# Keys' low parts on both halves of the partitions: attention products over full rows in a hybrid three-branch block

## The chip, the cores and the metric

The kernel runs on one core of a Trainium2 chip. The metric is the device time of one execution in microseconds (us), the median of several runs. The core's engines are named as in the profile: PE (TensorE, matrix products; PEld its weight loads), DVE (VectorE), ACT (ScalarE), POOL (GpSimd) and SP (SyncE, which here only issues DMAs).

## The reference

512 tokens behind 16 meta tokens, 1024 features, one layer, float32. Three attention branches read one projection of the normed input; their outputs are gated, projected and summed, and a convolutional gated feed-forward follows.

```python
def _stick_breaking(q, k, v):            # sb: 4 heads of 64
    z = einsum('bqhd,bkhd->bhqk', q, k) * scale
    log_1m_beta = where(key < query, log_sigmoid(-z), 0.0)
    between = cumsum(log_1m_beta, reverse) - log_1m_beta
    w = where(key < query, exp(log_sigmoid(z) + between), 0.0)
def _indexed_sparse_attention(...):      # sp: 4 heads; 132 keys per query, by an index score
    score = einsum('bqj,bqjk->bqk', w_ix, relu(einsum('bqjd,bkd->bqjk', q_ix, k_ix)))
    _, sel = top_k(score, top_k)         # then softmax(q k * scale + bias) over sel, times v
def _differential_attention(...):        # df: 4 heads, two maps each
    p = softmax(q1 k1 * scale + bias) - lam * softmax(q2 k2 * scale + bias)   # times v
merged = sum(sigmoid(g + b) * (y @ w_br)) over the three;  h = h + merged @ w_out
h = h + (silu(conv(u @ w_gate)) * (u @ w_val)) @ w_down
```

## The kernel before

Features lie on partitions, tokens on columns. For float32 accuracy every operand is split in a high part (rounded to the fast type `F32R`) and a low part, and a dense product is three passes: high times high, weights' high times low, weights' low times high (`mm3`). A dense tile is 8 k-tiles in 3 passes for each half of the tokens, with a new 128 x 128 weight tile loaded for every product of 256 to 264 columns.

TensorE runs in the order in which the code emits. `PLAN` gives the order of the dense tiles: projections of the units sb0, sb1 (two stick-breaking heads each), df0 to df3 (one differential head, two maps), sp0, sp1 (two sparse heads), gates, and branch outputs. Between a dense tile's products, generators ("streams") emit the attention's work, when a rough clock kept at emission says that their operands will be there (a margin `SLACK` of 1800 ns). The top-k of the sparse branch (`topk_stream`) runs on DVE beside the sb units. Weights come in chunks of 128 x 1024 on SP's queue (`wr<-wpk`), three buffers deep; ACT makes the high part (`wh`), POOL or DVE the low part (`wl`), which frees the buffer for a later load.

The attention of a unit goes like this. `q_stream` and `k_stream` (lines 635 to 666) split the projected queries and keys and move halves of 64 partitions by DMA on SP's queue (`move`, line 629): each head's queries become high and low parts above each other, (h, l) on 128 partitions; keys become (h0, h0), (h1, h1) and one tile (l0, l1), in `qk` tiles. `scores` (line 728) then makes two products per piece of a query block:

```python
mm(out, q[:, c0:c0 + m], (k0, k1)[e][:, o:o + n], start=True, stop=False)   # 128 rows: (h+l) of q, h of k
mm(out, q[rr, c0:c0 + m], kl[rr, o:o + n], start=False, stop=True)          # 64 rows: h of q, l of k
```

Each of the 16 score heads (2 for each unit; of a df unit the two maps) has pieces of 16 columns (the two meta queries), 144, 272, 400 and twice 264 (the blocks of 128 queries against the keys so far). DVE reads the scores, adding a mask (`smask`, for sb) or the bias (`W`). `value_stream` (line 855) transposes the weights on PE, the meta queries' 2 x 16 (`ws[i]`, tile `pm`) among them, and multiplies them with the values; the first of these products is over the meta keys (`pm,vm`): 64 rows for the paired heads of sb and sp, 96 rows for df.

Of the kernel before, what the change touches and what calls it, by code (L numbers as in the profile page):

```python
# [15 lines left out]
P = 128  # L16
D = 1024
T = 528            # meta tokens and real tokens
NM = 16
Q0 = 14            # first token whose mixer output is needed (the convolution reaches back two)  # L20
TQ = T - Q0        # 514 queries
HQ = TQ - 256      # 258: two meta queries and query blocks 0 and 1
# [11 lines left out]
# columns of the packed small parameters  # L34
# [4 lines left out]
# chunks of [128, 1024] in the packed weights  # L39
# [4 lines left out]
# the mixer's dense products in order: the projections of two heads' worth of a branch, four tiles  # L44
# of gates, half the columns of a branch's output
# [10 lines left out]
def tile_kernel(ctx: ExitStack, tc, hT, wpk, par, bias, yT):  # L56
# [3 lines left out]
    # ------------------------------------------------------------- order of emission  # L60
    # TensorE runs in the order in which its instructions are emitted here: dense products, with
    # the matmuls of other streams of work between them. A rough clock of the engines tells when a
    # stream's operands will be there, so that its matmuls come no earlier.
# [4 lines left out]
    SLACK = 1800    # from an operand's making by the clock to its matmul  # L68
    BSL = 500       # from a bank's last reading by the clock to its next use
    PACE = 12000    # for a round of the top-k  # L70
    TKS = 10000     # from the index part's making to its first product
    PRI = 100       # by how many instructions an evacuation goes ahead
    SET = 2200      # by how much earlier than SLACK the other engines' dependent steps come
    HVW = 1000      # VectorE's handicap against GpSimd for the weights' low parts
    HV = 500        # and for other differences
# [28 lines left out]

    def sub(out, a, b, hv=HV):
        """a - b in SBUF on VectorE, or on GpSimd where that is free sooner"""
        t = clock["P"]
        tv = max(clock["V"], t) + V.cost(out) + hv
        e = G if max(clock["G"], t) + G.cost(out) < tv else V
        e.tensor_tensor(out, a, b, OP.subtract)  # L110
# [16 lines left out]
    # ------------------------------------------------------------------ pools  # L127
# [13 lines left out]
    def bank(tag):  # L141
        """a PSUM bank, when one is free by the clock"""
        while sum(h["t"] + BSL > clock["P"] for h in held[tag]) >= banks[tag]:
            yield
        h = {"t": math.inf}
        held[tag].append(h)
        return ps.tile([P, 512], F32, tag=tag, bufs=banks[tag], name="ps" + tag), h
# [4 lines left out]
    # Slots that several streams of work share. A slot is taken here before the instructions  # L152
    # that fill it are emitted and given back after the last that reads it is, so an engine that
    # runs in the order of emission can't wait for one that is given back later.
    caps = {"tmp": 13, "qk": 10, "v": 2, "y": 8, "W": 3, "pt": 6, "ptm": 2}
# [29 lines left out]
    # ------------------------------- streams, which run between a dense product's matmuls  # L185
# [14 lines left out]
    def side_by_side(gens):  # L200
        """several streams in one; what each returns"""
# [16 lines left out]
    def settle(more=0):  # L218
        """until what the stream has emitted is done"""
        c = cur[0]  # L220
        while clock["P"] < c["t"] + more + SLACK:
            yield

    def ease(most=3000):
        """while VectorE is far behind"""
# [13 lines left out]
    # -------------------------------------------------------------- constants  # L239
    prm = const.tile([P, NPAR], F32, name="prm")  # L240

    def pc(c):
# [16 lines left out]
    # causal mask of a query block of 128 against columns c, the key at c standing at c - 400  # L259
    # from the block's first query  # L260
    cmask = const.tile([P, T], F32, name="cmask")
    G.memset(cmask, 0.0)
    G.affine_select(cmask, cmask, pattern=[[-1, T]], compare_op=OP.is_ge, fill=NEG, base=400,
                    channel_multiplier=1)
    smask = const.tile([P, T], F32, name="smask")
    G.memset(smask, 0.0)
    G.affine_select(smask, smask, pattern=[[-1, T]], compare_op=OP.is_gt, fill=NEG, base=400,
                    channel_multiplier=1)
    # the two meta queries (14 and 15) against the meta keys
# [4 lines left out]
    # ------------------------------------------------------- weights, streamed  # L274
# [34 lines left out]
    def mm3(out, prs, xh, xl, start=True, stop=True):  # L309
        """out += w^T x for the tiles j of chunk k and k-tiles kt of x, in three exact passes"""  # L310
# [13 lines left out]
    HALF = ((0, TH), (TH, TH))           # all tokens  # L324
    HALQ = ((0, HQ), (HQ, 256))          # queries, counted from token Q0

    # ------------------------------------------------ the input, and its norm's factors
# [16 lines left out]
    # the order that gives TensorE work from the first tile of the input on  # L344
# [21 lines left out]
    def step(k, ds, halves, q0, kt):  # L366
        """one k-tile of a tile of all its columns"""
# [12 lines left out]
    # the first two tiles go along with the input's arrival  # L380
# [17 lines left out]
    def rstd(dst, st, y0, a, now=True):  # L398
        """dst = (v + eps)^-0.5 from st = -v/2 in PSUM: Exp and Ln, then a Newton step"""
# [15 lines left out]
    # ------------------------------------------------ factors from the small parameters  # L415
# [6 lines left out]
    # -lambda of the differential attention on every partition  # L422
# [10 lines left out]
    # ------------------------------------- relative bias, by how far a key lies from the query  # L433
    tab = dram.tile([8, NREL], F32, name="tab")
    gd = [dram.tile([P, NREL], F32, name=f"gd{h}") for h in range(8)]
    braw = const.tile([97, 8 + NREL], F32, name="braw")
    nc.gpsimd.dma_start(braw, bias)

    def bias_stream():
# [3 lines left out]
        for e, r in enumerate(brd):  # L443
            # the table's high and low parts above each other, and the buckets of half the distances
# [14 lines left out]
        # a copy for each query, for the steps along which bias_tile reads  # L459
# [5 lines left out]
    def bias_tile(h):  # L465
        """[p, c]: the bias of query p against the key at column c (that is key c - 400 from the
        block's first query), or -1e30 where the key lies ahead"""
# [5 lines left out]
    # ----------------------------------------------------- dense tile of tokens  # L473
# [14 lines left out]
    # ---------------------------------------------------------------- index part  # L488
# [34 lines left out]
    for g in range(2):  # L523
# [15 lines left out]
        # the high, low and again the high parts of each head above each other, by way of DRAM  # L539
# [7 lines left out]
    # Each query's TOPK keys of the best score. Of the first block's 144 keys, the 144 - TOPK of the  # L547
    # least score are found instead: its scores are kept negated, and from the last key to the
    # first, since of equal scores the later key's counts as the lower.
# [10 lines left out]
    def topk_stream():  # L560
# [40 lines left out]
        # 0 where a key was taken, -1e30 elsewhere  # L601
# [5 lines left out]
    # ----------------------------------- after the projections of a unit of attention  # L607
    def headnorm(raw, n, gain, mat):
        """times gain over the root mean square of the rows that mat groups"""
# [622 lines left out]
```

## Time and profile before

| what | before |
|---|---|
| median of 3 runs | 931.87 us (929.49 to 934.09) |
| span of the profiled execution, first to last instruction | 928.0 us |
| busy in the span | PE 901.2 us (97%), DVE 559.4 (60%), ACT 456.7 (49%), POOL 314.5 (34%) |
| mean granted TensorE clock | 0.996 of full speed |
| weight chunks on SP's queue | 131 of 512 KB, 3.5 us from issue to landing |
| moves of key halves, `qk<-qk` of 132 KB | 24, 3.0 us from issue to landing |

The span is 3.9 us under the median; the two differ by what lies around the first and the last instruction and by the spread of the runs. Ends of products on PE are modelled in the profile, so the cost of a product is read from the starts: from its own to that of the next.

### The profile page before, as it was taken

Reading aid. Unit: us, or ns where it says so; the run is one execution under the profiler, and the core shown is the slowest. Engines: PE = TensorE matmul, PEld = TensorE weight load, DVE = VectorE, ACT = ScalarE, POOL = GpSimd, SP = SyncE. Lnnn points to the kernel's source line nnn. Section 1 sums busy time; section 2 is a strip of 40 time slices with the busy share of each in tenths; the row PEclk is TensorE's granted clock in tenths of the full one; section 3 lists DMA queues with packets and bytes.
Section 4 is the critical chain, followed back from the end, with each engine's and each line's share of the span. In section 5 each row is a group of like instructions: output and inputs, shape, how many; then the busy total and the mean of one; then the engine's idle time right before and its main releaser. Section 6 shows DMA issues by size and latency. Waiting matters only on the chain.

```text
span 928.0 us, 15349 instructions
## 1 busy us (share of the span) xinstructions
PE 901.2 (97%) x6054; PEld 814.3 (88%) x6054; DVE 559.4 (60%) x1129; ACT 456.7 (49%) x848; POOL 314.5 (34%) x185
## 2 busy tenths in 40 slices
PE   7989989899999999999998999999999999999998
PEld 6987988799998889988998999999999999888886
DVE  6599999985578655797437445555555555422221
ACT  7476686668377787644545444333333333311110
POOL 2433232343433424666235323344444333200100
PEclk9999999999999999999999999999999999999999
DMA  6584112142333212331222532223223233333330
GB/s 227 149 237 156 47 69 69 48 125 66 101 104 92 82 63 80 99 97 48 68 78 87 178 91 91 92 91 91 91 91 91 92 96 95 106 113 102 114 102 23
DMA packets 30439, 91.44 MB, mean 99 GB/s; under 512 B 3929, under 2 KB 4073, under 8 KB 30368
## 3 DMA queue, kind: packets, MB, share of 16 engines
q1 hardware_dynamic: 29648, 88.05, 31.0%
q0 software_dynamic: 720, 2.42, 0.9%
q8 instruction: 47, 0.77, 0.3%
q14 instruction: 24, 0.20, 0.1%
HBM read 80.88 MB, written 5.86 MB: 93 GB/s over the span
## 4 chain that ended last, share of the span: by engine, by line
PE 77%; DVE 14%; DMA 4%; ACT 2%; issue 1%; SPq 1%; POOL 0%; DVEq 0%; POOLq 0%; ACTq 0%
PE psd L179 52%; PE psw L179 23%; DVE tmp L97 7%; DVE work L97 2%; DVE m L97 2%; PE psw L183 2%; ACT tmp L97 1%; DMA qd<-tmp 1%; DVE G L97 1%; DMA qk<-qk 1%; DVE pm L97 1%; DMA wr<-wpk 1%; DVE pt L97 1%; DMA qst<-qd 1%; DMA gd<-tab 1%
## 5 line engine op out<-in xcount | busy, mean ns | idle before, releaser
L97 POOL TENSOR_TENSOR wl<-wr,wh 128x1024 fp32r<-128x1024 f32 x75 | 181.3, 2418 | 347.7 <-ACT wh L97 226.7
L97 ACT CAST wh<-wr 128x1024 fp32r<-128x1024 f32 (+2 forms) x137 | 139.2, 1018 | 178.4 <-PE psd L179 123.6
L179 PE MATMUL psd<-xh,wh 128*128 128x258 f32 (+2 forms) x792 | 119.5, 291 | 3.7 <-DVE tmp L97 2.5
L179 PE MATMUL psd<-xh,wl 128*128 128x258 f32 (+2 forms) x792 | 118.6, 290 | 0.0
L179 PE MATMUL psd<-xl,wh 128*128 128x258 f32 (+2 forms) x792 | 118.5, 290 | 0.0
L97 DVE TENSOR_TENSOR wl<-wr,wh 128x1024 fp32r<-128x1024 f32 (+3 forms) x62 | 72.3, 1168 | 69.4 <-PE psd L179 60.2
L179 PEld LDWEIGHTS psd<-xh,wh 128*128 128x128 f32 x792 | 103.8, 189 | 7.5 <-DVE tmp L97 1.8
L179 PEld LDWEIGHTS psd<-xh,wl 128*128 128x128 f32 x792 | 103.1, 189 | 3.3
L179 PEld LDWEIGHTS psd<-xl,wh 128*128 128x128 f32 x792 | 103.5, 190 | 2.9 <-issue 0.2
L97 ACT ACTIVATE tmp<-tmp 128x528 f32<-128x528 f32 (+7 forms) x154 | 69.7, 475 | 23.1 <-DVE tmp L97 20.5
L97 POOL TENSOR_TENSOR ft<-ft 128x512 f32<-128x512 f32 x22 | 46.5, 2115 | 82.5 <-DVE ft L97 79.1
L97 DVE SCALAR_TENSOR_TENSOR ft<-ft,prm 128x512 f32<-128x512 f32 x44 | 58.2, 1324 | 20.3 <-ACT ft L97 19.6
L179 PE MATMUL psw<-qk 128*128 128x400 f32 (+4 forms) x192 | 55.8, 339 | 2.3 <-DVE tmp L97 1.6
L179 PEld LDWEIGHTS psw<-qk 128*128 128x128 f32 (+1 forms) x192 | 32.2, 168 | 19.9 <-issue 6.2
L179 PE MATMUL psw<-uh,wh 128*128 128x256 f32 (+2 forms) x264 | 47.0, 320 | 0.0
L179 PE MATMUL psd<-ul,wh 128*128 128x258 f32 (+2 forms) x264 | 46.9, 319 | 0.0
L179 PE MATMUL psw<-ul,wh 128*128 128x256 f32 (+2 forms) x264 | 46.9, 319 | 0.0
L179 PE MATMUL psd<-uh,wl 128*128 128x258 f32 (+2 forms) x264 | 46.9, 319 | 0.0
L179 PE MATMUL psw<-uh,wl 128*128 128x256 f32 (+2 forms) x264 | 46.8, 319 | 0.0
L179 PE MATMUL psd<-uh,wh 128*128 128x258 f32 (+2 forms) x264 | 46.8, 319 | 0.0
L179 PE MATMUL psd<-ah,wl 128*128 128x512 f32 x176 | 45.6, 395 | 0.0
L179 PE MATMUL psd<-ah,wh 128*128 128x512 f32 x176 | 45.6, 395 | 0.0
(195 smaller groups left out, 1645.8 us busy)
## 6 DMA issues: line engine op xcount, KB each, us to landing
wr<-wpk SPq DMA_DIRECT2D x131, 512.0 KB, 3.5
qk<-qk SPq DMA_DIRECT2D x24, 132.0 KB, 3.0
gd<-tab SPq DMA_DIRECT2D x8, 328.0 KB, 5.2
tmp<-hT SPq DMA_DIRECT2D x8, 264.0 KB, 6.8
W<-gd POOLq DMA_DIRECT2D x8, 264.0 KB, 4.2
qk<-tmp SPq DMA_DIRECT2D x16, 128.5 KB, 2.6
hm<-hT SPq DMA_DIRECT2D x8, 257.0 KB, 3.8
yT<-ft SPq DMA_DIRECT2D x8, 256.0 KB, 2.1
```

The costliest lines, as they stand in the source:

```text
L97: return f(out, *a, **k)
L179: PE.matmul(out, lhsT, rhs, **k)
L183: PE.transpose(out, x, ident[:x.shape[0], :x.shape[0]])
```

## The change

The keys' low parts get the same treatment as the high ones: two tiles, (l0, l0) and (l1, l1), made by three more moves for each unit, and the second product of `scores` runs over all 128 rows (the queries' low part now also meets the keys' low part). A unit holds six `qk` tiles instead of five, and the pool two more. The meta keys' product takes all 96 rows of its tiles, whose other rows are zero. The meta queries' weights live in eight fixed tiles of 128 rows (`pmw`, zero below the second row), and a product with two columns of the identity takes the place of their transpose. One causal mask, a column wider, serves both branches: `smask` is `cmask` read one column on. The raw bias table moves to a slot of the gates' tiles.

```diff
-    caps = {"tmp": 13, "qk": 10, ...}
+    caps = {"tmp": 13, "qk": 12, ...}
-    cmask = const.tile([P, T], F32, name="cmask")
+    cmask = const.tile([P, T + 1], F32, name="cmask")
...
-    smask = const.tile([P, T], F32, name="smask")
-    G.memset(smask, 0.0)
-    G.affine_select(smask, smask, pattern=[[-1, T]], compare_op=OP.is_gt, fill=NEG, base=400, channel_multiplier=1)
+    smask = cmask[:, 1:]
...
-    braw = const.tile([97, 8 + NREL], F32, name="braw")
+    braw = ap_.tile([97, 4, TQ], F32, tag="G", bufs=4, name="braw").rearrange("p a b -> p (a b)")[:, :8 + NREL]
...  k_stream
-        yield from wait("qk", 3)
-        a, b, l = qtile(), qtile(), qtile()
+        yield from wait("qk", 4)
+        a, b, l, m = qtile(), qtile(), qtile(), qtile()
         S.copy(a, raw)
         sub(l, raw, a)
-        move(b[64:128], a[64:128])
-        move(b[0:64], a[64:128])
-        move(a[64:128], a[0:64])
+        for x, y in ((a, b), (l, m)):
+            move(y[64:128], x[64:128])
+            move(y[0:64], x[64:128])
+            move(x[64:128], x[0:64])
...  scores
-        q, (k0, k1, kl) = unit["q"][e], unit["k"]
-        rr = slice(64 * e, 64 * e + 64)
-        mm(out, q[:, c0:c0 + m], (k0, k1)[e][:, o:o + n], start=True, stop=False)
-        mm(out, q[rr, c0:c0 + m], kl[rr, o:o + n], start=False, stop=True)
+        q, kh, kl = unit["q"][e], unit["k"][e], unit["k"][2 + e]
+        mm(out, q[:, c0:c0 + m], kh[:, o:o + n], start=True, stop=False)
+        mm(out, q[:, c0:c0 + m], kl[:, o:o + n], start=False, stop=True)
...  weights of the meta queries
+    pmw = [ap_.tile([P, NM], F32, tag=f"pmw{j}", bufs=1, name=f"pmw{j}") for j in range(8)]
+    for t in pmw:
+        G.memset(t, 0.0)
-            return ap_.tile([2, NM], F32, tag="pm", bufs=8, name="pm")
+            pmw.append(pmw.pop(0))
+            return pmw[-1]
...  value_stream
-                transpose(t[:NM, o:o + m], ws[i][:m, :NM])
+                if i < 0:
+                    mm(t[:NM, o:o + 2], ws[i], ident[:, 0:2], start=True, stop=True)
+                else:
+                    transpose(t[:NM, o:o + P], ws[i][:, :NM])
...
-                mm(y[:, :W], vm[:64, e], pm[:64, :W], start=True, stop=False)
+                mm(y[:, :W], vm[:, e], pm[:, :W], start=True, stop=False)
```

On PE, ACT and DVE the order of the instructions stays what it was, but for four index-score products that come three dense products later, and one weight split that goes from POOL to DVE, both before the first unit's scores; on POOL two loads of bias tiles come a little later among the weight splits. What moves is SP's queue. In it, the moves of df0's keys (`qk` tiles to `qk` tiles of 64 x 528) with the weight loads around them (`wr`) read so before; the words in brackets are what an issue waits for, earlier DMAs (`DMAHW`), PE, ACT or POOL:

```order
L294 DMA wr19_2559<-wpk 128x1024 [waits DMAHW2_49,Pool_49]
L629 DMA qk_2506<-qk_2505 64x528 [waits PE_49,Activation_49]
L629 DMA qk_2506<-qk_2505 64x528
L629 DMA qk_2505<-qk_2505 64x528 [waits DMAHW2_49,DMAHW3_49,DMAHW1_49,Pool_49]
L294 DMA wr20_2621<-wpk 128x1024 [waits DMAHW4_49,Pool_49]
L294 DMA wr51_2740<-wpk 128x1024 [waits Pool_49]
```

And with the change:

```order
L292 DMA wr19_2570<-wpk 128x1024 [waits DMAHW0_49,Pool_49]
L627 DMA qk_2513<-qk_2512 64x528 [waits PE_49,Activation_49]
L627 DMA qk_2513<-qk_2512 64x528
L627 DMA qk_2515<-qk_2514 64x528 [waits DMAHW1_49,Pool_49]
L627 DMA qk_2515<-qk_2514 64x528 [waits DMAHW2_49]
L627 DMA qk_2512<-qk_2512 64x528 [waits DMAHW7_49,DMAHW0_49]
L292 DMA wr20_2632<-wpk 128x1024 [waits DMAHW4_49,Pool_49]
L627 DMA qk_2514<-qk_2514 64x528 [waits DMAHW5_49,DMAHW2_49,DMAHW1_49]
L292 DMA wr51_2749<-wpk 128x1024 [waits DMAHW6_49,Pool_49]
```

The low parts' two first moves stand behind the high parts' first two, and their last one stands behind the load of chunk 20. At sp0's keys, the same queue before:

```order
L629 DMA qk_4123<-qk_4122 64x528 [waits PE_49,Activation_49]
L629 DMA qk_4123<-qk_4122 64x528 [waits DMAHW3_49]
L629 DMA qk_4122<-qk_4122 64x528 [waits DMAHW3_49,DMAHW4_49,DMAHW2_49,Pool_49]
L294 DMA wr11_4354<-wpk 128x1024 [waits Pool_49]
L294 DMA wr12_4473<-wpk 128x1024 [waits DMAHW6_49,DMAHW0_49,Pool_49]
```

And with the change:

```order
L627 DMA qk_4136<-qk_4135 64x528 [waits DMAHW1_49,PE_49,Activation_49]
L627 DMA qk_4136<-qk_4135 64x528 [waits DMAHW2_49]
L627 DMA qk_4138<-qk_4137 64x528 [waits DMAHW3_49,Pool_49]
L627 DMA qk_4138<-qk_4137 64x528
L627 DMA qk_4135<-qk_4135 64x528 [waits DMAHW5_49,DMAHW2_49,DMAHW1_49]
L292 DMA wr11_4369<-wpk 128x1024 [waits DMAHW6_49,Pool_49]
L627 DMA qk_4137<-qk_4137 64x528 [waits DMAHW7_49,DMAHW4_49,DMAHW3_49]
L292 DMA wr12_4488<-wpk 128x1024 [waits DMAHW0_49,Pool_49]
```

Here too the last move of the low parts comes behind a weight load, and that load behind two more moves than before.

## Rows read from the trace of the kernel before

**Rows 1.** First line of the page.

```profile
span 928.0 us, 15349 instructions
```

**Rows 2.** Busy time by stretch (from:to us): length, engines' busy us, clock, DMA.

```profile
76.00:174.00 98.00, 89.76 (x649) 80.32 (x649) 97.39 (x227) 71.46 (x153) 25.70 (x12) 0.98 0.20 65
203.00:380.00 177.00, 176.24 (x1300) 161.92 (x1298) 112.57 (x296) 125.07 (x274) 65.62 (x39) 1.00 0.29 86
398.00:446.00 48.00, 47.49 (x334) 41.54 (x335) 38.69 (x107) 21.16 (x52) 28.03 (x21) 1.00 0.22 70
```

**Rows 3.** Chain that ended last, by line: stretches 76:174, 203:380, 380:398, 398:480.

```profile
by line: DVE tmp L97 41.4%; DVE work L97 19.6%; DVE m L97 17.2%; DVE pt L97 5.4%; DVE G L97 5.1%; DMA gd<-tab 4.8%; DVE pm L97 3.8%; ACT tmp L97 2.6%; issue 1.7%; ACT wh L97 1.0%; ACT pm L97 0.7%; DVE vt L97 0.6%; PE psw L179 0.3%; DVE vm L
by line: PE psd L179 61.6%; PE psw L179 20.5%; DVE tmp L97 6.3%; PE psw L183 4.8%; issue 2.4%; ACT tmp L97 1.5%; DVE r L97 1.4%; ACT wh L97 0.6%; DVE vt L97 0.4%; ACT qk L97 0.4%; DVE pm L97 0.3%; DVE mx L97 0.0%; ACTq L97 0.0%
by line: DVE tmp L97 29.6%; ACT tmp L97 19.2%; POOL tmp L97 17.1%; issue 15.7%; DVE pm L97 6.7%; ACT wh L97 5.7%; ACT y L97 3.5%; POOL y L97 2.5%; DVE r L97 2.0%; DVE G L97 1.8%; DVE mx L97 0.6%; DVEq L97 0.1%; POOLq L97 0.1%
by line: PE psd L179 71.9%; PE psw L179 19.7%; PE psw L183 7.9%; DVE tmp L97 1.7%; DVE pm L97 0.5%; issue 0.1%
```

**Rows 4.** Timeline of PE: start us, us, form (rows*columns), count of merged products.

```profile
69.24 0.65 PE L179 MATMUL psd<-xl,wh 128*128 128x264 f32 x4
69.73 1.43 PE L179 MATMUL psw<-qk 128*2 128x16 f32 x6
71.09 0.51 PE L179 MATMUL psd<-xh,wl 128*128 128x264 f32 x2
...
410.27 1.35 PE L179 MATMUL psw<-qk 128*128 128x400 f32 x4
411.55 0.75 PE L179 MATMUL psd<-y,wl 128*128 128x256 f32 x4
412.14 1.12 PE L179 MATMUL psd<-y,wh 128*128 128x258 f32 x8
413.19 0.38 PE L179 MATMUL psw<-pm,vm 64*128 64x258 f32 x1
413.50 0.70 PE L179 MATMUL psw<-qk 128*128 128x264 f32 x2
414.13 0.62 PE L179 MATMUL psd<-y,wl 128*128 128x258 f32 x3
```

**Rows 5.** Score products by stretch: 76:174, 203:380, 380:398, 398:480; meta keys' of 398:480.

```profile
L179 PE MATMUL psw<-qk x42: 168/383/543, 77.1 to 154.6; 128*128 128x264 f32 x8, 64*128 64x264 f32 x8, 128*128 128x400 f32 x4, 64*128 64x400 f32 x4
L179 PE MATMUL psw<-qk x96: 167/368/448, 202.9 to 348.8; 128*128 128x264 f32 x16, 64*128 64x264 f32 x16, 128*2 128x16 f32 x8, 64*2 64x16 f32 x8
L179 PE MATMUL psw<-qk x14: 168/333/443, 385.5 to 397.0; 128*2 128x16 f32 x2, 64*2 64x16 f32 x2, 128*128 128x144 f32 x2, 64*128 64x144 f32 x2
L179 PE MATMUL psw<-qk x34: 168/385/450, 402.0 to 441.0; 128*128 128x264 f32 x8, 64*128 64x264 f32 x8, 128*128 128x400 f32 x3, 64*128 64x400 f32 x3
L179 PE MATMUL psw<-pm,vm x8: 380/382/392, 400.2 to 471.6; 64*128 64x258 f32 x4, 64*128 64x256 f32 x4
```

**Rows 6.** Timeline of DVE about 203 us, where its backlog ends.

```profile
202.30 0.75 DVE L97 TENSOR_TENSOR G<-psd,rs 128x258 f32<-128x258 f32 x2
203.25 0.16 DVE L97 CUSTOM_DVE_ANT_0 pm<-psw,W 2x16 f32<-2x16 f32 x1 [0.21 <-PE psw L179]
```

**Rows 7.** Timeline of SP's queue at df0's keys.

```profile
196.15 3.46 SPq L629 DMA_DIRECT2D qk<-qk  x3
199.93 0.33 SPq L294 DMA_DIRECT2D wr<-wpk  x1
```

**Rows 8.** Waits (us in total, times, longest) and DMA issues (count, KB, us to landing).

```profile
SPq L629 <- DMA qk<-qk: 22.2, 12, 3.3
...
ACT wh L97 <- PE psd L179: 123.6, 46, 6.0
...
qk<-qk SPq DMA_DIRECT2D x24, 132.0 KB, 3.0
```

**Rows 9.** DVE's adds of sb's mask: ns min/median/max, first and last start.

```profile
L97 DVE TENSOR_TENSOR tmp<-psw,smask x20: 285/414/566, 77.3 to 159.1; 128x264 f32<-128x264 f32 x8, 128x144 f32<-128x144 f32 x4, 128x272 f32<-128x272 f32 x4, 128x400 f32<-128x400 f32 x4
```

More of the change, by code (lines that the diff above doesn't have):

```diff
@@ L150, in drop @@
         h["t"] = cur[0]["t"]
-    caps = {"tmp": 13, "qk": 10, "v": 2, "y": 8, "W": 3, "pt": 6, "ptm": 2}
+    caps = {"tmp": 13, "qk": 12, "v": 2, "y": 8, "W": 3, "pt": 6, "ptm": 2}
     banks = {"d": 3, "w": 5}
@@ L258, in tile_kernel @@
     V.memset(one, 1.0)
-    cmask = const.tile([P, T], F32, name="cmask")
+    cmask = const.tile([P, T + 1], F32, name="cmask")
     G.memset(cmask, 0.0)
-    G.affine_select(cmask, cmask, pattern=[[-1, T]], compare_op=OP.is_ge, fill=NEG, base=400,
+    G.affine_select(cmask, cmask, pattern=[[-1, T + 1]], compare_op=OP.is_ge, fill=NEG, base=400,
                     channel_multiplier=1)
-    smask = const.tile([P, T], F32, name="smask")
-    G.memset(smask, 0.0)
-    G.affine_select(smask, smask, pattern=[[-1, T]], compare_op=OP.is_gt, fill=NEG, base=400,
-                    channel_multiplier=1)
+    smask = cmask[:, 1:]
     smeta = const.tile([2, NM], F32, name="smeta")
@@ L656, in k_stream @@
             yield from headnorm(raw, n, gain, blk)
-        yield from wait("qk", 3)
-        a, b, l = qtile(), qtile(), qtile()
+        yield from wait("qk", 4)
+        a, b, l, m = qtile(), qtile(), qtile(), qtile()
         S.copy(a, raw)
         sub(l, raw, a)
-        move(b[64:128], a[64:128])
-        move(b[0:64], a[64:128])
-        move(a[64:128], a[0:64])
+        for x, y in ((a, b), (l, m)):
+            move(y[64:128], x[64:128])
+            move(y[0:64], x[64:128])
+            move(x[64:128], x[0:64])
         give("tmp")
-        unit["k"] = (a, b, l)
+        unit["k"] = (a, b, l, m)
         unit["t"] = max(unit.get("t", 0), cur[0]["t"] + 5000)
@@ L849, in weight_stream @@
                 jobs.append((unit, hf, e, heads, ws, cur[0]["t"] + SLACK))
-        give("qk", 5)
+        give("qk", 6)
         for w in unit.get("W", ()):
@@ L874, in value_stream @@
             for i in BLOCKS[hf]:
-                m = 2 if i < 0 else P
-                transpose(t[:NM, o:o + m], ws[i][:m, :NM])
-                o += m
+                if i < 0:
+                    mm(t[:NM, o:o + 2], ws[i], ident[:, 0:2], start=True, stop=True)
+                else:
+                    transpose(t[:NM, o:o + P], ws[i][:, :NM])
+                o += 2 if i < 0 else P
             S.copy(pm[0:NM, :o], t[:NM, :o])
```

## Prediction

> **What bounds the kernel now.** The first view to read is the page: the span is 928.0 us [rows 1], and PE is busy in 97% of it. That share is an average, and modelled, so the second view is the chain of work that ended last, cut by stretch [rows 3], beside the engines' busy time by stretch [rows 2]. The reader is to see that the attention part has two limits. From 76 to 174 us, where the sb units run beside the top-k, the chain is DVE's nearly throughout (PE has 0.3%), and DVE is busy 97.39 of 98.00 us. From 203 to 380 us, the df units, PE has 61.6 + 20.5 + 4.8 = 87% of the chain, and DVE is busy 112.57 of 177. From 380 to 398 us the chain runs over DVE, ACT and POOL and has no PE. From 398 to 480 us, the rest of the sp units, PE has 71.9 + 19.7 + 7.9 = 99.5%. After 480 us nothing that the change touches is left.
>
> The third view is PE's timeline [rows 4], read from start to start. Four dense products of 264 columns take 69.73 - 69.24 = 0.49 us, 0.122 each, or 0.46 ns a column. The six score products behind them (a product over 128 rows and one over 64 for 16, 144 and 272 columns) take 71.09 - 69.73 = 1.36 us for 864 columns in all, 1.6 ns a column. So a product over 64 rows between ones over 128 costs more than its columns, at its start and at its end.
>
> **The change part by part.**
>
> *Scores.* At 410.27 a pair of 400 and a pair of 264 columns take 411.55 - 410.27 = 1.28 us, at 413.50 a pair of 264 takes 0.63 [rows 4]. A head has one pair each of 16, 144, 272 and 400 columns and two of 264, so it takes 1.36 + 1.28 + 0.63 = 3.27 us now. With all products over 128 rows I price them as dense ones: 2 x (0.067 + 0.125 + 0.184 + 2 x 0.122) us for the five wide pairs, and 0.05 for a product of 16 columns, which no row shows alone; together 1.34 us. That saves 1.93 us a head, 0.16 for each of its 12 products. The bounds are nothing (the low part's product over 128 rows steps as now) and this; I take the dense step, since the new product has the dense products' form, type and weight tile. For 192 products the sum is 31 us.
>
> *Meta keys' product, sb and sp.* Its start comes 413.19 - 412.14 = 1.05 us after that of eight dense products, 0.09 more than their 0.96, and it takes 413.50 - 413.19 = 0.31 instead of 0.12: 0.28 us each, 16 of them, 4.5 us.
>
> *Meta queries' transposes.* Twelve, over 2 rows. Leaving that form saves the 0.09 us at the start, and the new product over 128 rows has two columns of full float32. I take 0.05 us each, between nothing and 0.15: 0.6 us.
>
> All of it would be 36 us. What counts is where it lies [rows 5], times PE's share of the chain there [rows 3]:
> - Up to 174 us: 42 score products (6.7 us), the six at 69.73 (1.0) and half of the meta keys' (2.2). DVE has 0.61 us of idle time, its work stays, and its backlog lasts to 203 us: its first wait for PE (0.21 us) stands at 203.25, right behind two evacuations back to back [rows 6]. Also, df0's first scores at 202.9 [rows 5] need keys that come out of DVE's queue. I take 0.5 us.
> - 203 to 380 us: 96 products, 15.4 us, by 0.87: 13.4 us.
> - 380 to 398 us: 14 products, 2.2 us, and no PE in the chain: nothing.
> - 398 to 480 us: 34 products (5.4 us) and 8 meta keys' (2.2), by 0.995: 7.6 us. DVE is busy 38.69 of 48.00 us in the first part of it [rows 2], which then becomes 42 us: 92%. For waits that this makes I take 1 us off.
>
> *Moves.* 24 more, of 132 KB each. Issues on SP cost PE nothing, but the last move of each set waits for the first ones: 22.2 us in 12 such waits before, 1.9 each, 3.3 at most [rows 8]. Queued behind it are the weight loads. They are hidden as long as ACT's casts wait for PE (123.6 us in 46 waits [rows 8]) and not for a load. At df0 the last added move stands behind the load of chunk 20, issued at 199.93 [rows 7]; it goes out at 200.3 and lands, 3.0 us after [rows 8], at about 203.3, when the first scores want it at 202.9. So 0.4 us are lost there, and I take 0.5 for all units; the bound is 3.3 on each of eight, 26 us.
>
> *The rest.* The masks, the zeroed tiles and the bias table's slot are POOL's in the first 6 us, beside the input's loads, and cost nothing; without that cover they are about a microsecond. Reading the mask one column on is 20 adds of 0.41 us on DVE [rows 9], in the stretch where DVE is the limit: were each a tenth slower, 0.8 us would be lost; I take nothing.
>
> The sum: 0.5 + 13.4 + 7.6 + 0.2 (transposes on the chain) - 1 - 0.5 = 20 us. The span becomes 908 us. The median of the runs stands 3.9 us above the profiled span, and I leave that as it is: 931.9 - 20 = 912 us.
>
> **The rivals.**
>
> *The step does not change.* In the trace, weight loads of dense products over the same 128 rows do run beside the product before, or eight could not follow each other in 0.96 us [rows 4]. If that failed for the score products, nothing would be saved and the moves would cost up to a few us: 932 us. Chance 0.04.
> The Trainium skill ("TensorE: Matmul & The Clock Gate", Part 3, on what overlaps and what doesn't) says that a weight load overlaps a running product only when the two use different groups of rows; by that, products that all use every row would gain nothing, which is this rival. The dense rows at 0.122 us disagree with it.
>
> *All of the 36 us arrive.* DVE would have to be no limit between 76 and 174 us, against its 97.39 us of work in 98.00. At best DVE's order loosens and the low shares are too pessimistic: below 901 us, worked out 896. Chance 0.08.
>
> *DVE takes most of it.* With PE faster by 8% from 203 us on, evacuations come late and the products behind them wait. DVE's 64% in the df stretch speaks against it, its 81% from 398 us for it. Half of 13.4 and of 7.6 us would be left: 921 to 925 us. Chance 0.06.
>
> *Slower: the moves hold up the weights.* Each set blocks SP's queue once more; a dense chunk of 48 products lasts 48 x 0.122 = 5.9 us, and a load that comes late stops PE at once. To end 0.5% above the median, PE would have to stand still for 20 + 5 = 25 us more, 3.1 for each of the eight units, close to the longest wait seen, 3.3 [rows 8], and with no slack before it. ACT's casts waiting on PE speak against that. Then 937 us or more. Chance 0.04.
>
> A word on the clock: in the stretch from 76 to 174 us its mean is 0.98 [rows 2], so for about 4 us of the 98 it stood at the lower level, 1.2 GHz, which took some 2 us of PE's work; PE had 8.2 us without a product in that stretch. It will have some 9 us more of them, so the clock may fall again; four more such falls would stay hidden behind DVE.
>
> **How the numbers follow.** The likeliest case, with 0.78, is the sum by stretch, 901 to 921 us, and its middle 912 is the prediction. To 901 it takes shares of one after 203 us and no new waits; to 921, half the gain. The range 900 to 922 us leaves out most of the full gain (0.08), half of the third rival, and the two cases of no gain (0.08). A measurement of this kernel can tell about 0.5%, 4.7 us, from no change: slower 0.04, the same 0.05 (the first rival and the tail of the third), faster 0.91.
>
> **What would show it.** In the profile after: score products over 128 rows only, six of them at the first unit in about 0.5 us instead of 1.36, pairs of 264 columns in 0.25; meta keys' products over 96 rows stepping 0.12. From 76 to 174 us DVE still busy all the time, PE idle some 9 us more and waiting for DVE, the end of DVE's backlog still near 203 us. The end of the attention, and with it the span, some 20 us earlier, most of it won between 203 and 370 us and from 398 us on. Wrong would be: steps of 0.3 us that stay; PE stopped in front of the first scores of a unit by a move; casts waiting for loads; DVE without idle time after 203 us.

## The result

| | before | after |
|---|---|---|
| median of the runs, us | 931.65 (929.49 to 934.09, 4 runs) | 918.96 (915.45 to 922.29, 4 runs) |
| ratio | 1 | 0.987, 95% interval 0.9835 to 0.9904 |
| span of the profiled execution, us | 928.0 [rows 1] | 918.0 |

The change wins 12.7 us; forecast were 20, in a range of 10 to 32 us won. The direction and the range held, the size was too large by 7 us. (The two profiled executions differ by 10.0 us only: the span of before lies 3.7 us under the median in this table, that of after 1.0 us under its own.) The page of the kernel after (its first line, and PE's busy time with share and instructions) shows PE with less work and less of the span:

```profile
span 918.0 us, 15420 instructions
PE 876.1 (95%) x6066; PEld 813.8 (89%) x6066; DVE 559.1 (61%) x1130; ACT 455.6 (50%) x848; POOL 312.0 (34%) x190
```

PE's timeline of the kernel after (start us, us, form, count) at the place that [rows 4] show of before:

```profile
405.29 0.76 PE L179 MATMUL psw<-qk 128*128 128x400 f32 x4
405.89 0.64 PE L179 MATMUL psd<-y,wl 128*128 128x256 f32 x4
406.37 1.12 PE L179 MATMUL psd<-y,wh 128*128 128x258 f32 x8
407.33 0.28 PE L179 MATMUL psw<-pm,vm 96*128 96x258 f32 x1
407.45 0.41 PE L179 MATMUL psw<-qk 128*128 128x264 f32 x2
407.70 0.65 PE L179 MATMUL psd<-y,wl 128*128 128x258 f32 x4
```

Read from start to start, a pair of 400 and a pair of 264 columns take 0.60 us instead of 1.28, a pair of 264 takes 0.25 instead of 0.63, the meta keys' product 0.12 instead of 0.31, and the eight dense products before it 0.96 instead of 1.05. These are the dense steps that the prediction priced.

So the step came, and yet 7 us are missing. The place of the loss is seen by following the same products through both traces: the score products and the meta keys' of the kernel after, by stretch (first the df units', then the sp units' first 14 and last 34, count, ns, first and last start us; the last row holds all meta keys' products).

```profile
L179 PE MATMUL psw<-qk x96: 170/286/522, 202.9 to 343.1; 128*128 128x264 f32 x32, 128*2 128x16 f32 x16, 128*128 128x144 f32 x16, 128*128 128x272 f32 x16
L179 PE MATMUL psw<-qk x14: 170/300/428, 379.5 to 393.6; 128*2 128x16 f32 x4, 128*128 128x144 f32 x4, 128*128 128x272 f32 x4, 128*128 128x400 f32 x2
L179 PE MATMUL psw<-qk x34: 170/284/428, 397.5 to 432.8; 128*128 128x264 f32 x16, 128*128 128x400 f32 x6, 128*2 128x16 f32 x4, 128*128 128x144 f32 x4
L179 PE MATMUL psw<-pm,vm x24: 279/283/416, 91.8 to 462.8; 96*128 96x258 f32 x12, 96*128 96x256 f32 x12
```

Against [rows 5]: the df units' first product starts at 202.9 us in both, so these two traces show nothing won up to there. Their last one comes 348.8 - 343.1 = 5.7 us earlier, sp's first one 385.5 - 379.5 = 6.0, its last one 441.0 - 432.8 = 8.2, the last meta keys' 471.6 - 462.8 = 8.8. Some 5.7 us in the df stretch, where 13.4 were forecast: that is the missing part.

The second view is PE's waits in that stretch, 203 to 380 us (what PE waited for: us in total, times, longest), of the kernel after:

```profile
PE psw L183 <- DVE mx L97: 3.8, 1, 3.8
PE psw L179 <- DMA qk<-qk: 2.3, 2, 1.9
```

and of the kernel before, one wait in 177 us:

```profile
PE psw L183 <- DVE mx L97: 0.8, 1, 0.8
```

So PE stands still for 5.3 us more. The third view is the granted clock by stretch of the kernel after (from:to, length, busy us of the engines, the clock, DMA), where the last two rows lie behind the wait of 3.8 us:

```profile
203.00:380.00 177.00, 170.61 (x1346) 166.78 (x1344) 117.57 (x305) 128.16 (x285) 69.11 (x41) 0.97 0.36 99
198.00:220.00 22.00, 20.07 (x157) 19.63 (x157) 13.61 (x55) 15.13 (x30) 7.28 (x4) 0.92 0.36 105
282.00:286.00 4.00, 3.53 (x18) 3.20 (x19) 2.97 (x12) 3.95 (x12) 1.33 (x1) 0.50 0.87 229
282.47:288.00 5.53, 5.53 (x28) 5.20 (x29) 2.92 (x11) 4.85 (x14) 1.20 (x1) 0.53 0.71 201
```

Before, the clock was 1.00 in that whole stretch [rows 2]. Now it stood at its lower level, 1.2 GHz, for a while behind each of the two stops, which took 0.08 x 22 + 0.47 x 5.53 = 4.4 us of PE's work. 5.7 + 5.3 + 4.4 = 15.4 us: the 96 products did give their 0.16 us each, and 9.7 us of it went to two stops and what the clock did behind them.

### The profile page after: what moved, and what is told of

The parts are those of the page before. It is cut to its first block, busy times and chain, and to the rows that moved or that the text cites. A ratio compares the mean times of both kernels' runs of the same rounds, so it can differ in the third digit from the quotient of the medians.

```text
span 918.0 us, 15420 instructions
## 1 busy us (share of the span) xinstructions
PE 876.1 (95%) x6066; PEld 813.8 (89%) x6066; DVE 559.1 (61%) x1130; ACT 455.6 (50%) x848; POOL 312.0 (34%) x190
## 4 chain that ended last, share of the span: by engine, by line
PE 50%; DVE 2%; ACT 0%; POOL 0%; issue 0%; ACTq 0%; DVEq 0%
PE psd L179 34%; PE psw L179 16%; DVE tmp L97 1%; DVE G L97 1%; DVE ml L97 0%; PE psw L183 0%; POOL wl L97 0%; ACT wh L97 0%; POOL tmp L97 0%; ACT tmp L97 0%; PE st L179 0%; DVE ft L97 0%; DVE pt L97 0%; DVE pmw L97 0%; DVE r L97 0%
## 5 line engine op out<-in xcount | busy, mean ns | idle before, releaser
L97 POOL TENSOR_TENSOR wl<-wr,wh 128x1024 fp32r<-128x1024 f32 x74 | 179.2, 2422 | 350.7 <-ACT wh L97 257.2
L97 DVE TENSOR_TENSOR wl<-wr,wh 128x1024 fp32r<-128x1024 f32 (+3 forms) x63 | 74.5, 1184 | 70.6 <-PE psd L179 60.6
L179 PEld LDWEIGHTS psd<-xl,wh 128*128 128x128 f32 x792 | 106.3, 195 | 0.5
L179 PEld LDWEIGHTS psd<-xh,wl 128*128 128x128 f32 x792 | 105.4, 193 | 1.0
L97 DVE SCALAR_TENSOR_TENSOR ft<-ft,prm 128x512 f32<-128x512 f32 x44 | 58.6, 1333 | 20.3 <-ACT ft L97 19.6
L179 PE MATMUL psw<-qk 128*128 128x400 f32 (+4 forms) x192 | 37.5, 301 | 15.0 <-DVE tmp L97 6.4
L179 PE MATMUL psd<-al,wh 128*128 128x512 f32 x176 | 45.8, 396 | 0.0
```

What stands on the lines that cost most here:

```text
L97: return f(out, *a, **k)
L179: PE.matmul(out, lhsT, rhs, **k)
```

## The experiments

A note for all of them: spans of the same kernel differ by 2 us and more before 203 us (the kernel after starts its df units at 202.9 us in one profiled execution, at 201.2 in another), so places are compared by the length of a stretch, first to last score product, and whole kernels by the medians.

**The parts of the change.** `a1_whole` is the kernel after once more, beside its parts. `a2_rest_only` takes the meta products, the mask and the table's slot, with scores and moves as before. `a3_moves_only` makes the six moves and keeps the low product over 64 rows (the mask and the table's slot are the new ones, the meta products the old). `a4_zero_low` has products over 128 rows without any added move: the low parts stand in two tiles whose other half is zero, made by two subtractions of half the rows.

```diff
 a3, against the kernel after, scores:
-        mm(out, q[:, c0:c0 + m], kl[:, o:o + n], start=False, stop=True)
+        mm(out, q[rr, c0:c0 + m], kl[rr, o:o + n], start=False, stop=True)
 a4, against the kernel after, k_stream:
-        sub(l, raw, a)
-        for x, y in ((a, b), (l, m)):
-            move(y[64:128], x[64:128])
-            move(y[0:64], x[64:128])
-            move(x[64:128], x[0:64])
+        sub(l[0:64], raw[0:64], a[0:64])
+        nc.gpsimd.tensor_tensor(m[64:128], raw[64:128], a[64:128], OP.subtract)
+        move(b[64:128], a[64:128])
+        move(b[0:64], a[64:128])
+        move(a[64:128], a[0:64])
...
```

> The whole change again, beside the three partial ones. Theory (late moves and half-clock stretches ate part of the gain): 916 to 922 us, PE waiting some 2 to 3 us before the first scores of df0 and of sp0, with a granted clock of half speed in a stretch right after each. Rival (those waits were chance of one execution): the waits are missing in this trace, and the time is near 912.

> Scores and moves as before; only the meta keys' product over 96 rows, the meta queries' product, the one mask and the bias table's slot are changed. Theory: 8 meta keys' products of 0.28 us after 398 us count, the others lie under DVE: 2 to 3 us gained, 928 to 930 us. Rival (these are worth as much as the scores): 922 or less. If the start of the kernel is later by about 1.3 us, as in the whole change, the new places of mask and table cause it.

> The keys' low parts are moved as in the change (three more moves a unit), with the one mask and the bias table's slot, but the low parts' product stays over 64 rows and the meta products as before. Theory: the moves cost waits at the first scores of df0 and sp0 and a little at the start, 1 to 5 us lost, 933 to 937 us. Rival (moves cost nothing, the waits of the change came from PE being faster): 930 to 932 us and no wait for a move in the trace.

> Scores over 128 rows as in the change, but the low parts need no move: each head's low part is written onto its own half of the partitions of a tile whose other half holds zeros (one more subtraction on POOL for each unit, three moves fewer). Theory: the waits at df0 and sp0 (4.9 us) and the half-clock stretches behind them (3.4 us of PE's time) go, 6 to 8 us less than the whole change: 911 to 913 us. Rival (PE would have waited for DVE there anyway): no less than 917.

| kernel | median us (runs from, to) | ratio to before, 95% | df scores, first to last start | length |
|---|---|---|---|---|
| before | 931.9 (928.52 to 934.57) | 1 | 202.9 to 348.8 | 145.9 |
| a1_whole | 918.38 (914.12 to 919.84) | 0.9856 (0.9821 to 0.9891) | 201.2 to 340.9 | 139.7 |
| a2_rest_only | 929.0 (928.07 to 930.3) | 0.9972 (0.9957 to 0.9987) | 204.8 to 350.9 | 146.1 |
| a3_moves_only | 930.2 (928.89 to 931.08) | 0.9985 (0.9973 to 0.9997) | 203.1 to 349.0 | 145.9 |
| a4_zero_low | 917.02 (915.76 to 918.45) | 0.9848 (0.9816 to 0.988) | 204.8 to 341.2 | 136.4 |

`a1_whole` shows the same stops again: 2.05 us at df0's low product, 3.77 for DVE, 2.7 at sp0's scores, and a clock of 0.50 from 282 to 284 and from 382 to 384 us, behind the last two; so they weren't chance. The rest alone wins some 2.6 us by the ratio, as its theory had it; the prediction had 2.4 (the meta keys' from 398 us on, and the transposes). The moves alone cost nothing that can be measured, against their theory of 1 to 5 us. But `a3` doesn't test whether PE has to wait for them: its low products read rows 0 to 63 of `l` and rows 64 to 127 of `m`, and the last move writes rows 64 to 127 of `l`, which none of them reads. There this move is issued at 200.62, as in the kernel after, and PE, which comes to df0's scores at the same time, runs all six products at once:

```profile
203.06 1.44 PE L179 MATMUL psw<-qk 128*2 128x16 f32 x6
```

In the kernel after the low product reads all 128 rows, so it needs the last move too. SP's queue (start us, us) and PE's timeline of the kernel after at df0:

```profile
200.74 0.46 SPq L627 DMA_DIRECT2D qk<-qk  x1
204.90 0.33 SPq L292 DMA_DIRECT2D wr<-wpk  x1
```

```profile
202.91 0.17 PE L179 MATMUL psw<-qk 128*2 128x16 f32 x1
205.02 0.74 PE L179 MATMUL psw<-qk 128*2 128x16 f32 x5 [1.93 <-DMA qk<-qk]
205.60 1.82 PE L179 MATMUL psd<-xh,wl 128*128 128x258 f32 x8
```

The first product, on the high parts, runs at 202.91; the second, on the low parts, waits until the last move has landed, which was issued at 200.74 behind the load of chunk 20. Behind the stop, eight dense products of 258 columns take 207.22 - 205.60 = 1.62 us instead of 0.97 (206.42 - 205.45 in the next kernel). In the kernel with zero-padded low parts PE doesn't stop there, and the six products take 205.45 - 204.84 = 0.61 us (1.36 before [rows 4]):

```profile
204.84 0.17 PE L179 MATMUL psw<-qk 128*2 128x16 f32 x1
...
205.45 1.13 PE L179 MATMUL psd<-xh,wl 128*128 128x258 f32 x8
206.42 0.17 PE L179 MATMUL psw<-qk 128*2 128x16 f32 x1
```

Its df stretch is 140.2 - 136.4 = 3.8 us shorter than that of the kernel after: 1.9 of the stop and about the same by the clock, which is 1.00 there. The whole kernel gained less, 1.4 to 1.9 us by the medians, which is within the intervals, and the other wait, of 3.8 us for DVE, stayed. So the time is the rival's (no less than 917), not the theory's 911 to 913. Where the rest of the 3.8 us went isn't settled; in its trace the first score product of all stands at 71.2 us, where the two executions of the kernel after have 69.0 and 68.2.

**Is DVE's top-k what hides the rest?** Both kernels with 3 instead of 17 rounds of the top-k; the other 14 are left out.

```diff
-        for r in range(-(-TOPK // 8)):
+        for r in range(3):
```

> The kernel before with 3 of the 17 rounds of the top-k (the other 14 are left out, so the mask of the sb units holds fewer keys). The partner of the next run; what is read is their difference. If DVE is the limit from 76 to 198 us, this kernel itself becomes faster, since most of DVE's work there is gone: by 20 to 60 us.

> The kernel after with the same 14 of 17 rounds left out. Theory (what the sb units win is swallowed by DVE, 76 to 198 us): without that limit their 42 score products and meta keys come through as well, and the difference to the run before this one grows from 12.7 to 18 to 22 us. Rival (the gain of the sb units is lost for another reason, PE's order or the moves): the difference stays at 11 to 14 us.

Measured: 926.4 us (922.54 to 931.18) for before, 906.08 (905.62 to 907.11) for after, 20.3 us apart. That is the theory's number, but not from the theory's place, and the two traces show only part of it: their spans are 920.9 and 905.3 us, 15.6 apart, since the profiled execution of before took 922.8 us, near the lowest of its runs. The df units' scores of these two kernels, before and then after (count, ns, first and last start):

```profile
L179 PE MATMUL psw<-qk x96: 167/376/450, 196.1 to 342.6; 128*128 128x264 f32 x16, 64*128 64x264 f32 x16, 128*2 128x16 f32 x8, 64*2 64x16 f32 x8
```

```profile
L179 PE MATMUL psw<-qk x96: 170/284/432, 195.2 to 328.7; 128*128 128x264 f32 x32, 128*2 128x16 f32 x16, 128*128 128x144 f32 x16, 128*128 128x272 f32 x16
```

Up to df0's first product nothing is won, though DVE has far less to do: from the first score product of all it is 196.1 - 69.9 = 126.2 us before and 195.2 - 68.9 = 126.3 after. So the sb units' gain doesn't come through without the top-k either (the stretch of their 42 later products is 2.9 us shorter, 76.0 to 146.4 us against 77.2 to 150.5, and that is gone at df0). From 66 to 197 us PE stands still 5.1 us in the kernel before and 11.6 in the one after, in short waits for ACT and DVE most of all: the gain became waiting there. Taking most of the top-k away won only 4 to 5 us in the kernel before, not 20 to 60, because PE is the limit right behind DVE there: 94.35 us of work in the same 98 us.

```profile
76.00:174.00 98.00, 94.35 (x701) 85.31 (x700) 74.29 (x158) 75.83 (x164) 28.47 (x14) 1.00 0.23 73
```

What grew is the df stretch: 146.5 us before, 133.5 after, 13.0 won, as the prediction had it (13.4). In this kernel PE has no wait for a bank of scores there. So the theory of this pair falls, and the question becomes why PE stops at 278 us in the kernel after and not here; the part on that stop answers it.

**Are the dependent products emitted too soon?** The margin of the emission's clock is 3000 ns instead of 1800, in the kernel with zero-padded low parts and in the kernel before.

```diff
-    SLACK = 1800
+    SLACK = 3000
```

> The kernel after with zero-padded low parts in place of the added moves, and with 3000 instead of 1800 ns between the making of an operand by the emission's clock and the product that reads it. Theory (PE's waits at 278, 385 to 389, 411 and 423 us come because dependent products are emitted too soon behind their operands, now that PE is faster): these waits and the half clock behind the one at 278 shrink, and the time is 909 to 914 us. Rival (the work of DVE itself is the limit there, whatever the order): 917 us or more.

> The kernel before with the same 3000 ns. Theory: it had few such waits, so little is won, 929 to 933 us, and the difference to the run with 3000 ns and faster scores grows to 17 to 22 us. Rival: it wins as much as that run does.

Measured: 937.19 us (934.94 to 938.05) and 953.07 (952.41 to 953.78), both slower than the kernel before, and 15.9 us apart. The theory falls. The later the attention's products come, the fewer dense ones are left to stand beside them at its end: from 398 to 446 us they are 191 and 75, where the kernel before had 241. By stretch, of the two kernels in that order:

```profile
369.00:398.00 29.00, 17.58 (x89) 13.23 (x89) 21.48 (x70) 20.50 (x58) 12.39 (x14) 0.80 0.27 69
398.00:446.00 48.00, 44.80 (x306) 39.57 (x307) 39.08 (x110) 26.21 (x67) 23.29 (x21) 0.87 0.13 40
```

```profile
369.00:398.00 29.00, 25.82 (x118) 19.26 (x117) 18.11 (x59) 20.11 (x56) 8.36 (x10) 0.72 0.27 75
398.00:446.00 48.00, 43.22 (x210) 31.75 (x209) 39.18 (x122) 27.96 (x78) 19.99 (x20) 0.78 0.09 21
```

Of all products there are 306 and 210 in 48 us, where the kernel before had 334 [rows 2], at a clock of 0.78 to 0.87.

**The stop at 278 us.** The timelines of DVE and POOL in the kernel after show what holds the bank for which PE waits:

```profile
278.64 2.95 DVE L97 SCALAR_TENSOR_TENSOR tmp<-tmp,prm 128x528 f32<-128x528 f32 x1
281.51 0.41 DVE L97 TENSOR_TENSOR tmp<-psd,rs 128x256 f32<-128x256 f32 x1
281.85 0.56 DVE L97 CUSTOM_DVE_ANT_0 tmp<-psw,W 128x400 f32<-128x400 f32 x1
```

```profile
278.69 2.34 POOL L97 TENSOR_TENSOR wl<-wr,wh 128x1024 fp32r<-128x1024 f32 x1 [6.14 <-ACT wh L97]
```

DVE's product of the key norm (`headnorm`'s last line) takes 2.95 us, where such products have a median of 0.77, while POOL subtracts a weight chunk's low part. Behind it DVE reads the scores only at 281.85, and PE, which needs their bank for a value transpose, starts that at 282.47, after 3.77 us. In the kernel before, DVE's product starts at 278.65 and takes 2.98; but PE then was some 3 us behind (the score products ahead of the stop begin at 280.41 there and at 277.65 here), and waited 0.76 us:

```profile
278.65 2.98 DVE L97 SCALAR_TENSOR_TENSOR tmp<-tmp,prm 128x528 f32<-128x528 f32 x1
```

```profile
282.52 0.28 PE L183 MATMUL psw<-ident,tmp 128*16 128x128 f32 x1 [0.76 <-DVE mx L97]
```

The Trainium skill ("SBUF — State Buffer", the section "SBUF: two separate sides" and "Who interferes with whom" in it) states that a DVE instruction with two SBUF inputs contends with a GpSimd instruction that reads SBUF, that whichever comes first has the shared ports for its whole length, and that the other blocks. The trace agrees that one blocks: 2.34 + 0.77 = 3.1 us against 2.95. Which came first it doesn't tell here, since DVE's start is recorded 0.05 us ahead. Where POOL's is clearly ahead, the kernel before has a DVE instruction of 128x1 that takes 0.16 us elsewhere and here ends with POOL's subtraction, 272.58 and 272.56:

```profile
270.18 2.38 POOL L97 TENSOR_TENSOR wl<-wr,wh 128x1024 fp32r<-128x1024 f32 x1 [5.78 <-PE psd L179]
270.52 2.06 DVE L97 TENSOR_TENSOR r<-r,nlam 128x1 f32<-128x1 f32 x1
```

In the kernel after without most of the top-k, the two instructions miss each other, and PE has no stop there:

```profile
266.08 0.76 DVE L97 SCALAR_TENSOR_TENSOR tmp<-tmp,prm 128x528 f32<-128x528 f32 x1
267.07 2.41 POOL L97 TENSOR_TENSOR wl<-wr,wh 128x1024 fp32r<-128x1024 f32 x1 [3.83 <-ACT wh L97]
```

Two kernels test it. `c1_after_low26` gives this one chunk's low part to DVE, seven rows behind that product in its queue. `c4_after_busy` puts 24 products more, whose result is thrown away, in front of the transpose.

```diff
 c1, prep:
-        sub(wl, r, wh, HVW)
+        if k in (26,):
+            book("G", G.cost(wl))
+            nc.vector.tensor_tensor(wl, r, wh, OP.subtract)
+        else:
+            sub(wl, r, wh, HVW)
 c4, v_stream, for the fifth unit, ahead of the meta tokens' transpose:
+            d = psd()
+            for _ in range(24):
+                PE.matmul(d[:, :264], xh[:, 0, :P], xh[:, 0, :264], start=True, stop=True)
```

> The kernel after, in which one chunk's low part (the one that GpSimd subtracts at 278.7 us, beside VectorE's product of 128x528) is subtracted on VectorE instead, seven rows later in its queue. Theory: VectorE's product took 2.95 us there instead of 0.77 because GpSimd's subtraction ran beside it; without that, the bank for which PE waits 3.77 us comes free some 2.2 us sooner, PE's wait is 1.2 to 2 us, the half clock behind it becomes shorter or goes, and 2 to 5 us are won: 914 to 917 us. Rival (the wait ends by something else, or VectorE's own subtraction gives the gain back): within 1 us of the kernel after, 918 to 920.

> The kernel after with 24 more dense products of 264 columns (2.9 us; their result is thrown away) right in front of the product at which PE stands for 3.77 us at 278.7. Theory (the half clock from 281 to 287.6 us follows from that standing still): PE stands for about 0.9 us, the half clock there goes, PE is 3 us further at 290 us, and the time is 915 to 917 us. Rival (the clock falls there whatever PE does in these microseconds, or the bound is elsewhere): no change, or up to 0.5 us more, 918 to 920.

`c1`: 914.89 us (914.09 to 916.87), ratio 0.9828 (0.9807 to 0.985), 3.5 to 4 us under the two medians of the kernel after, though the intervals overlap. DVE's product takes 0.77 us, PE's stop is 1.58 instead of 3.77, and the df stretch is 338.1 - 201.6 = 136.5 us, 3.7 shorter. The timelines of DVE and of PE, and the stretch behind the stop:

```profile
277.16 0.77 DVE L97 SCALAR_TENSOR_TENSOR tmp<-tmp,prm 128x528 f32<-128x528 f32 x1
```

```profile
278.81 0.28 PE L183 MATMUL psw<-ident,tmp 128*16 128x128 f32 x1 [1.58 <-DVE mx L97]
```

```profile
280.00:282.00 2.00, 2.00 (x12) 1.67 (x11) 2.00 (x5) 1.35 (x4) 0.01 (x1) 0.50 0.86 192
282.00:286.00 4.00, 4.00 (x32) 3.94 (x31) 3.29 (x11) 3.17 (x9) 0.44 (x1) 0.93 0.81 218
```

The clock still falls, for a shorter time. The theory holds in each of its numbers, and the stretch of the trace, 3.7 us shorter, is its firmer evidence.

`c4`: 917.59 us (915.36 to 919.21), ratio 0.9851 (0.983 to 0.9872). Its PE doesn't stop at all, and its clock stays up:

```profile
276.96 3.04 PE L705 MATMUL psd<-xh 128*128 128x264 f32 x24
279.84 0.27 PE L183 MATMUL psw<-ident,tmp 128*16 128x128 f32 x1
```

```profile
282.00:286.00 4.00, 4.00 (x34) 3.94 (x33) 2.99 (x9) 2.26 (x7) 0.20 (x1) 1.00 0.88 240
```

It isn't the clean test that it was meant to be, because the collision went the other way in it: DVE's product took 0.77 us, and POOL's subtraction, begun 0.05 us behind it, took 2.98. (In the kernel after, too, DVE's is recorded 0.05 us ahead, and there DVE lost.) So this stop would have been about 1.6 us, as in `c1`, without the added products. Against `c1` it tells the clock's share: PE's transpose comes 1.5 us later behind the df units' first product (279.84 - 201.1 = 78.7 us, against 278.81 - 201.6 = 77.2), yet the df stretch is 338.4 - 201.1 = 137.3 us against 136.5: of the 1.5 us, 0.7 came back, and `c4` lost 0.5 more at 320.97 us, waiting for a move, so 1.2 did. By the two rows of `c1` its clock cost 0.50 x 2 + 0.07 x 4 = 1.3 us there. That PE's standing still brings the clock down is supported, not settled: the time lies between the two expectations, and the runs overlap with those of the kernel after.

**Both losses at once, and the same edit in the kernel before.**

```diff
 d1: a4_zero_low with c1's edit;  d2: the kernel before with c1's edit
```

> Zero-padded low parts in place of the added moves, and that one chunk's low part subtracted on VectorE instead of GpSimd. Theory (the stop at df0's first scores and the one at 278 us are two separate losses): both gains add, 917.0 less 3 = 912.5 to 915 us, and PE's wait at 278 us is 1 to 2 us instead of 3.9. Rival (what is won at 278 us is given back at a later stop): 916.5 us or more.

> The kernel before with the same chunk's low part on VectorE. Theory (the same collision stood in the kernel before, and PE, still busy with its scores, waited only 0.76 us for it): 0 to 1 us are won, 930 to 932 us. Rival (the edit helps any kernel, by less work on GpSimd or VectorE in general): it wins 3 us or more, 928.5 us or less.

`d1`: 914.01 us (913.58 to 914.84), ratio 0.9817 (0.98 to 0.9834), within the theory's 912.5 to 915 and the lowest median of the kernels that leave nothing out, though not to be told from `c1`. Its scores (here the low parts' products) run from 204.0 to 336.8:

```profile
L179 PE MATMUL psw<-lz,qk x48: 170/284/346, 204.0 to 336.8; 128*128 128x264 f32 x16, 128*2 128x16 f32 x8, 128*128 128x144 f32 x8, 128*128 128x272 f32 x8
```

That stretch is 132.8 us long, 13.1 shorter than before, where the sum had 13.4. The parts add: 5.7 in the kernel after, 3.8 without the late move, 3.7 without the collision, 13.2 together.

`d2`: 929.5 us (927.27 to 932.65, 12 runs), ratio 0.9978 (0.9964 to 0.9991), between the two expectations. In its trace the df stretch is 352.2 - 207.2 = 145.0 us, 0.9 shorter than before, as the theory had it; where the median's other 1.1 us come from isn't settled, and it is about the size of the interval.

## Why the prediction was right, and where its size was off

- **The step**: right. Pairs of 264 columns take 0.25 us, four products of 400 and 264 columns 0.60, the six of a head's first part 0.61, where 0.25, 0.61 and 0.48 were priced; the meta keys' product 0.12. In the df stretch the products gave 15.4 / 96 = 0.16 us each, as forecast. Weight loads of products over the same 128 rows run beside the product before, as the dense rows had it; the first rival is out.
- **Up to 174 us, 0.5 us**: about right. From the first score product of all to df0's first it takes 132.7 to 133.9 us in the four traces with the whole change's scores and 133.2 to 134.9 in the four that keep the old ones with the whole top-k and the margin of 1800 ns: about 1 us, within the scatter. That DVE's work hides the rest was the reason given; the pair without most of the top-k showed that it is not the whole reason, since nothing came through there either.
- **203 to 380 us, 13.4 us**: this is the term that failed in the kernel as it is. 5.7 us came. The sum took PE's share of the chain, 0.87, for what would be won, as if the other 13% stayed where they were. But DVE's chain of score reading, norm and bank at 278 us ran at the same times in both traces, so PE, coming 3 us earlier, only waited longer there: 3.77 us instead of 0.76. Without the late move and the collision (`d1`) 13.1 us came.
- **Moves, 0.5 us for all units**: too small, though the place was named rightly, and a stop of PE in front of a unit's first scores stood among the signs of being wrong. The wait at df0 was 1.9 us where 0.4 was worked out: the last move was issued at 200.74 instead of 200.3, and PE's next product came 205.02 - 200.74 = 4.3 us behind its issue instead of 3.0. sp0's keys cost 2.6 us more, below. By themselves the moves cost nothing, and ACT's casts wait 2.4 us in all for a weight load, against 1.5 before: the rival that they hold up the weights is out.
- **380 to 398 us, nothing; 398 to 480 us, 6.6 us**: from sp's first score product to the last meta keys' product it was 471.6 - 385.5 = 86.1 us and is 462.8 - 379.5 = 83.3, so 2.8 us. PE's waits in that stretch of the kernel after:

```profile
PE psw L179 <- DMA qk<-qk: 2.6, 1, 2.6
PE psw L179 <- DVE tmp L97: 2.2, 2, 1.2
PE psw L183 <- DVE pm L97: 0.5, 1, 0.5
PE psw L179 <- DVE pm L97: 0.4, 1, 0.4
```

  5.7 us against 1.0 before, and a clock of 0.92 from 376 to 398 us (1.8 us more), where the sum had 1 us for DVE and nothing for a move. In `d1`, without the moves, DVE's waits are longer instead (6.1 us), and the stretch is 82.9 us: there the third rival, DVE near its limit, is right.
- **The clock**: the prediction spoke of it only for the stretch that DVE hides. It fell behind the stops at 205 and 281 us too, where PE is the limit, and took 4.4 us. That term was missing. In the stretch that DVE hides it fell more than expected, to 0.93 of 98 us instead of 0.98, so that up to 5 us of what PE won there went to the clock:

```profile
76.00:174.00 98.00, 84.08 (x644) 80.91 (x642) 96.38 (x223) 71.18 (x153) 25.75 (x12) 0.93 0.27 78
```

- **What is left**: 8.8 us are won at the last meta keys' product, 10.0 in the span. From 500 to 512 us the kernel before had a clock of 0.86 in its profiled execution and the kernel after 1.00; the change touches nothing there. That the medians differ by 2.7 us more than the spans is the spread of the runs.

So the mechanism was right and the sum of the work too; what was mis-sized is the price of stops: 1.5 us in the sum, and in the trace 5.3 + 4.7 us of standing still and 4.4 + 1.8 us of lower clock.

## What to carry to other kernels

A gain on the engine that sets the end counts only up to the next moment at which it waits for another chain that doesn't move. So walk along the trace of before, look up at each stretch's dependent products how much slack their operands have (0.76 us of waiting is a sign that there is none), and take off what the gain so far exceeds it by; a share of the chain is too mild. A stop is then priced with what the granted clock does behind it, here some six tenths as much again as the stop itself. Where such a stop is found, look at the waited-for engine for an instruction that is several times longer than its like: moving one subtraction off POOL was worth 3.7 us of the stretch. And a test that adds a transfer without its reader, as `a3` does, can't show that the reader will wait for it.

## What the runs showed of the hardware

A DVE instruction with two SBUF operands, 0.77 us alone, took 2.95 us beside a POOL subtraction of 128 x 1024, or POOL's took 2.98 instead of 2.34 us; which of them blocked changed between kernels with the same recorded lead of 0.05 us. The stop of 1.58 us at the same transpose was followed by a clock of 0.50 in `c1` and of 1.00 in `d1`, as this row of `d1` shows:

```profile
278.00:282.00 4.00, 3.19 (x27) 2.95 (x27) 3.99 (x11) 3.36 (x9) 3.25 (x2) 1.00 0.31 68
```

What tells the two apart isn't settled. And products over 96 of 128 rows between ones over 128 step like dense ones, 0.12 us for 258 columns, where those over 64 rows cost 0.31.
